# GpSimd computes the low part of 32 of 338 half slabs of weights

## The chip, the cores and the metric

The kernel runs on one core of a Trainium2 chip. A time is the device time of one execution in microseconds. Before the change it is 1015.32 us, the median of three runs (1015.02 to 1015.72). The profile shows one further execution. In its lines PE is TensorE's matmul, PEld its weight load, DVE is VectorE, ACT is ScalarE, POOL is GpSimd, and SP the engine whose queue issues the DMA transfers.

## The reference

The program is a decoder trunk of two layers on one sequence of 256 positions and width 1024, all in fp32. A layer is a feed-forward block, a mixer and a second feed-forward block, each with a modulated input and a residual with layer norm:

```python
mod = c_act @ mod_w[l] + mod_b[l]
sh1, sc1, g1, sh2, sc2, g2, sh3, sc3, g3 = jnp.split(mod, N_MOD, axis=-1)
f = swiglu(modulate(x, sh1, sc1), ffn_in[l, 0], ffn_out[l, 0])
x = deepnorm_residual(x, f, g1, ln_g[l, 0], ln_b[l, 0], 0.5)
u = modulate(x, sh2, sc2)
m = even_mixer(u, ...) if l % 2 == 0 else odd_mixer(u, positions, ...)
x = deepnorm_residual(x, m, g2, ln_g[l, 1], ln_b[l, 1])
f = swiglu(modulate(x, sh3, sc3), ffn_in[l, 1], ffn_out[l, 1])
x = deepnorm_residual(x, f, g3, ln_g[l, 2], ln_b[l, 2], 0.5)
```

The mixer of layer 0 ("even") joins a gated linear recurrence (RG-LRU, with a causal convolution in front) with chunked gated linear attention; that of layer 1 ("odd") is latent attention with 8 heads. The modulation vectors (shift, scale and gate of every block) are products of one conditioning vector with a large matrix.

## The kernel before

Activations lie transposed, 128 channels on the partitions by 256 positions, so every product has a 128 x 128 block of weights as the stationary operand. Each fp32 product is made of three products of a narrower form: the weight and the activation are both split into a high and a low part, and `mm3` issues high x high, high x low and low x high (L431, L432, L433). The activation parts are `uhi`, `ulo` for a block's input and `hhi`, `hlo` for the hidden layer.

The weights of the whole trunk stand in HBM in the order in which they are used (`PLAN`), in slabs of 16 blocks. `Stream` brings them: `dma_to` loads a slab of 1 MB into one of six raw buffers (`wraw`), from SP's queue; `conv_to` splits it in two half slabs of 128 x 1024 each. ACT copies the raw half slab into the high part (`whi`, L353, five buffers), and DVE subtracts that from the raw values to give the low part (`wlo`, L354, five buffers). The first slab is used unsplit, which leaves 338 half slabs to split. `next` hands out blocks and asks for the splits four half slabs ahead. A half slab feeds 24 matmuls.

The modulation products are not matmuls. `mods_to` loads two blocks of `modw` into one raw buffer, from the same queue and at a pace set by a table (`MOD_TARGETS`), and notes them in `todo`; `reduce` has DVE multiply such a 128 x 1024 block with the conditioning vector and add along the row (L405, tile `junk`, followed by a short accumulator read). `conv_to` calls it after a split when the first block noted is due, and twice when more than four are waiting.

The rest of DVE's work stands between: the hidden layer's product `h` (L818) and its split (L507), the layer norm (tiles `yy`, `acc`, `v`; class `Boundary`, where B of L631 is a folded modulation row), and the mixers. In the even mixer these are the key and query products (L1101, L1102, and L1108 with tile `la`), the recurrence's steps on four channel blocks at a time (`ya`, L978 to L987), and the residual (`xh`, L759). PE's L1075 there takes the scores of one head from `la`. `EVEN_STEPS` is the order of the even mixer's steps, one letter each: decays, values, keys, queries, gates and so on.

A scheduler decides in which order an engine's instructions stand, by priorities and by its own estimates of time; a few chains are tied by hand (`queue_behind`). Each engine then works through its queue in order, waiting on semaphores of the others. GpSimd has 24 instructions in this kernel, memsets and selects for constants and masks, none of which takes two inputs.

Of the kernel before, what the change touches and what calls it, by code (L numbers as in the profile page):

```python
# [11 lines left out]
F32 = mybir.dt.float32  # L12
# [7 lines left out]
MULT, ADD, SUB, MAX, MIN = ALU.mult, ALU.add, ALU.subtract, ALU.max, ALU.min  # L20
# [22 lines left out]

SH, SC, GT = 0, 1, 2
PRE, PREU = 4, 1
UOFF = 100
GOFF = 150
LVEC = (5, 6, 7)
# [187 lines left out]
def trunk_kernel(ctx: ExitStack, tc: tile.TileContext, xT, cvec, pos, wst, modw, colsd,  # L236
                 rgw, wa2, outT):
    nc = tc.nc
    sync, act, vec, pool, pe = nc.sync, nc.scalar, nc.vector, nc.gpsimd, nc.tensor
# [21 lines left out]
    def T(pl, shape, dt=F32, tag=None, **kw):  # L261
        return pl.tile(shape, dt, tag=tag, name=nm(tag), **kw)
# [12 lines left out]
    def axps():  # L275
        return T(ps_ax, [P, 512], tag="ax")
# [7 lines left out]
    def col(name, i, n=1):  # L284
        o = COLS[name][0]
        return cols[:, o + i:o + i + n]
# [18 lines left out]
    class Stream:  # L305
# [4 lines left out]
        def __init__(self):  # L310
            self.pos = 0
            self.raw = {}
            self.conv = {}
            self.ndma = 0
            self.nconv = 0
            self.nmod = 0
            self.todo = []
            self.behind = None
            self.pause = False
            self.ahead = Stream.AHEAD  # L320
            self.tight = False
            self.after = None
            self.modcols = {}
# [13 lines left out]
        def conv_to(self, n):  # L337

            self.dma_to((n - 1) // 2 + Stream.RAW)
            W2 = Stream.HS * P  # L340
            while self.nconv < min(n, 2 * NSLAB):
                s = self.nconv
                if s < 2 * RAWSLABS:

                    self.conv[s] = (self.raw[s // 2][:, (s % 2) * W2:(s % 2 + 1) * W2], None)
                    if s % 2:
                        self.raw.pop(s // 2)
                    self.nconv += 1
                    continue
                hi = T(whi, [P, W2], F32R, tag="whi")  # L350
                lo = T(wlo, [P, W2], F32R, tag="wlo")
                raw = self.raw[s // 2][:, (s % 2) * W2:(s % 2 + 1) * W2]
                ia = act.activation(hi, raw, AF.Copy)  # L353
                i = vec.tensor_tensor(lo, raw, hi.bitcast(F32), SUB)  # L354
                self.last_conv = ia, i
                if self.behind is not None:
                    queue_behind(i, self.behind)
                self.conv[s] = (hi, lo)
                if s % 2:
                    self.raw.pop(s // 2)  # L360
                self.nconv += 1
                if self.todo and not self.pause and self.todo[0][2] <= s // 2:
                    self.reduce()
                    if len(self.todo) > 4 and self.todo[0][2] <= s // 2:
                        self.reduce()
# [56 lines left out]
    W = Stream()  # L422
# [12 lines left out]
    def queue_behind(i, j):  # L435
        tc.add_manual_dep(i.ins, j.ins.name, mybir.DependencyInfo(
            mybir.DependencyClass.NoSync, mybir.DependencyReason.DATA), reason="order")
# [167 lines left out]
    class Boundary:  # L605
# [134 lines left out]
        def u(self, k):  # L740
# [3 lines left out]
            self.done.add(k)  # L744
            with tc.high_priority(offset=UOFF):
                if k >= PRE:
# [175 lines left out]
    def even(l, prev):  # L922
        with tc.tile_pool(name=nm("even"), bufs=1) as ep, tc.tile_pool(name=nm("ew"), bufs=2) as ew:
# [91 lines left out]
            def decays():  # L1015
                for h in range(GH):
                    hsl = slice(h * SEQ, (h + 1) * SEQ)
                    zp = axps()
                    pe.matmul(zp[:, :SEQ], wa2t[:, h * GDK:(h + 1) * GDK], za, start=True, stop=True)
                    act.activation(la[:, hsl], zp[:, :SEQ], AF.Abs, bias=col("gla_ba", h))  # L1020
                    vec.tensor_scalar(lb[:, hsl], zp[:, :SEQ], col("gla_ba", h), 0.0, ADD, MIN)
                ta(la, la, AF.Exp, scale=-1.0)
                ta(la, la, AF.Ln, bias=one_c)
                vec.tensor_tensor(la, lb, la, SUB)
                for h in range(GH):
                    hsl = slice(h * SEQ, (h + 1) * SEQ)
                    vec.tensor_tensor_scan(bc[:, hsl], scmask, la[:, hsl], 0.0, MULT, ADD)
                ta(la, bc, AF.Exp, scale=1.0 / 16)
                b3, lb3 = (t.rearrange("p (n e c) -> p n e c", e=2, c=GC) for t in (bc, lb))
                vec.tensor_copy(last, b3[:, :, :, GC - 1])  # L1030
                vec.tensor_copy(dec, la.rearrange("p (n e c) -> p n e c", e=2, c=GC)[:, :, :, GC - 1])
                ta(lb3[:, :, 1], b3[:, :, 1], AF.Exp, scale=-1.0 / 16)
                for e, t in ((0, lb3), (1, b3)):
                    vec.tensor_tensor(t[:, :, e], last[:, :, e:e + 1].broadcast_to([P, 2 * GH, GC]), b3[:, :, e], SUB)
                    ta(t[:, :, e], t[:, :, e], AF.Exp, scale=1.0 / 16)
                ta(b3[:, :, 0], b3[:, :, 0], AF.Exp, scale=-1.0 / 16)
# [105 lines left out]
                return yahi, yalo  # L1142

            for step in EVEN_STEPS:
                if step == "d": decays()
                elif step == "k": keys()
                elif step == "q": queries()
                elif step == "v": values()
                elif step == "A": gla_state()
                elif step in "OP": gla_out("OP".index(step))  # L1150
                elif step in "RS":
                    ta.use("exp_and_others")
                    rglru(4 * "RS".index(step))
                elif step == "g": sgg = gates()
                elif step == "a": yahi, yalo = rg_gates()
# [6 lines left out]

            with tc.high_priority(offset=UOFF):
                s8 = ss.rearrange("p t h -> p (t h)")
# [35 lines left out]
    def odd(l, prev):  # L1200
        with tc.tile_pool(name=nm("odd"), bufs=1) as op_, tc.tile_pool(name=nm("ow"), bufs=2) as ow:
# [63 lines left out]
            for half in range(2):  # L1265
                hi, lo = W.next(*[(("kv_up",), 0, ("v", 4 * half + c)) for c in range(4)])
# [66 lines left out]
            def queries(n):  # L1333
                for _ in range(n):
                    if ahead:
                        query(*ahead.pop(0))
# [4 lines left out]
            def output(f, ks):  # L1341
                if not first:
                    first.append(mmps())
                for k in ks:
                    mm3(first[0][:, :SEQ], W.next((("odd_out",), k, f)), (ohi[:, k, :], olo[:, k, :]),
                        k == 0, k == KD - 1)

            queries(4)
            for i in range(MH + 2):
                if i < MH:  # L1350
# [16 lines left out]
            for f in range(KD):  # L1367
                if f == 0:
                    ps = first[0]
                    output(0, range(6, KD))  # L1370
                    bd.tile_out(f, ps[:, :SEQ])
                    continue
                ps = mmps()
                for k in range(KD):
                    mm3(ps[:, :SEQ], W.next((("odd_out",), k, f)), (ohi[:, k, :], olo[:, k, :]),
                        k == 0, k == KD - 1)
                    if f == 1 and k == KD // 2:
                        bd.shift_out()
                bd.tile_out(f, ps[:, :SEQ])
        return bd  # L1380

    bd = None
# [99 lines left out]
```

## Time and profile before

| what | before |
|---|---|
| median of three runs | 1015.32 us |
| the profiled execution | 1015.46 us |
| its span, first to last instruction | 1013.7 us |
| TensorE busy, granted clock | 998.4 us, 0.997 |
| VectorE busy | 877.4 us |
| ScalarE busy | 611.9 us |
| GpSimd busy | 4.6 us |

The page gives for each engine its busy time within the span, and for groups of instructions with one line, operation and tiles their number, their busy time, the mean of one in ns, the idle time ahead of them and what ended it. Busy times overlap, as the engines run side by side. A wait is named by what released it.

### The profile page before, as it was taken

What the parts mean: (1) busy time and instruction counts of PE and PEld (TensorE: products, weight loads), DVE (VectorE), ACT (ScalarE), POOL (GpSimd) and SP (SyncE); (2) the same over time, 40 slices, a digit from 0 to 9 for tenths busy, and PEclk for the clock granted to TensorE, in tenths of its full rate; (3) what the DMA queues carried; (4) which work ended last, traced back from release to release, by engine and by line L of the source; (5) the groups of instructions that cost most, each with busy time, mean ns of one, the idle gap of its engine ahead of it and who ended that gap; (6) DMA issues with size and microseconds to landing.
All of it is one profiled execution on the core that took longest, in us unless ns stands there. A gap on an engine that the chain in (4) does not pass through costs nothing.

```text
span 1013.7 us, 20595 instructions
## 1 busy us (share of the span) xinstructions
PE 998.4 (98%) x8368; PEld 977.2 (96%) x8368; DVE 877.4 (87%) x1502; ACT 611.9 (60%) x1026; POOL 4.6 (0%) x24
## 2 busy tenths in 40 slices
PE   8999999999999999999999999999999999999997
PEld 7999999998999999999999999999999999999995
DVE  6889999798999999999986899999788799666664
ACT  5656665678895766655555674454569776454542
POOL 0000000000000000000000000000000000000000
PEclk9999999999999999999999999999999999999998
DMA  9998699554467954799976469998843156656501
GB/s 332 415 403 329 258 352 333 203 208 176 157 250 303 360 194 174 269 380 389 345 294 248 165 255 388 321 337 327 285 166 126 45 193 251 254 219 246 189 20 42
DMA packets 37999, 258.56 MB, mean 255 GB/s; under 512 B 4352, under 2 KB 5632, under 8 KB 7568
## 3 DMA queue, kind: packets, MB, share of 16 engines
q1 hardware_dynamic: 37904, 257.25, 67.5%
q8 instruction: 65, 1.06, 0.4%
q14 instruction: 30, 0.25, 0.1%
HBM read 256.18 MB, written 1.05 MB: 254 GB/s over the span
## 4 chain that ended last, share of the span: by engine, by line
PE 84%; DVE 9%; DMA 3%; issue 2%; ACT 2%; SPq 0%; DVEq 0%; ACTq 0%
PE mm L432 25%; PE mm L433 25%; PE mm L431 25%; DVE wlo L354 3%; DMA wraw<-modw 3%; DVE junk L405 1%; PE mm L1120 1%; PE mm L1119 1%; PE mm L1121 1%; ACT whi L353 1%; DVE flat L987 0%; PE ax L432 0%; PE ax L431 0%; PE ax L433 0%; PE mm L841 0%
## 5 line engine op out<-in xcount | busy, mean ns | idle before, releaser
L354 DVE TENSOR_TENSOR wlo<-wraw,whi 128x1024 fp32r<-128x1024 f32 x338 | 409.0, 1218 | 74.3 <-ACT whi L353 73.4
L353 ACT ACTIVATE whi<-wraw 128x1024 fp32r<-128x1024 f32 x338 | 355.2, 1057 | 192.6 <-PE mm L432 147.8
L431 PE MATMUL mm<-uhi,whi 128*128 128x256 f32 x1624 | 448.7, 277 | 0.8 <-DVE h L818 0.8
L432 PE MATMUL mm<-ulo,whi 128*128 128x256 f32 x1624 | 448.6, 277 | 0.1
L433 PE MATMUL mm<-uhi,wlo 128*128 128x256 f32 x1624 | 448.4, 277 | 0.0
L431 PEld LDWEIGHTS mm<-uhi,whi 128*128 128x128 f32 x1624 | 304.3, 188 | 1.4 <-ACT whi L353 1.0
L432 PEld LDWEIGHTS mm<-ulo,whi 128*128 128x128 f32 x1624 | 304.9, 188 | 0.6 <-DVE ulo L753 0.3
L433 PEld LDWEIGHTS mm<-uhi,wlo 128*128 128x128 f32 x1624 | 304.8, 188 | 0.1
L431 PE MATMUL mm<-hhi,whi 128*128 128x256 f32 x704 | 194.4, 276 | 0.0
L433 PE MATMUL mm<-hhi,wlo 128*128 128x256 f32 x704 | 194.4, 276 | 0.0
L432 PE MATMUL mm<-hlo,whi 128*128 128x256 f32 x704 | 194.4, 276 | 0.0
L405 DVE CUSTOM_DVE_ANT_0 junk<-wraw,cact,cols 128x1024 bf16<-128x1024 f32 x136 | 173.5, 1276 | 6.6 <-DMA wraw<-modw 6.2
L433 PEld LDWEIGHTS mm<-hhi,wlo 128*128 128x128 f32 x704 | 132.2, 188 | 0.0
L432 PEld LDWEIGHTS mm<-hlo,whi 128*128 128x128 f32 x704 | 132.2, 188 | 0.0
L431 PEld LDWEIGHTS mm<-hhi,whi 128*128 128x128 f32 x704 | 132.2, 188 | 0.0
L506 ACT ACTIVATE hhi<-h 128x256 fp32r<-128x256 f32 x88 | 36.0, 413 | 63.5 <-DVE h L818 63.5
L682 ACT ACTIVATE ysq<-yy 128x256 f32<-128x256 f32 x42 | 17.4, 415 | 44.6 <-DVE yy L678 44.1
L818 DVE SCALAR_TENSOR_TENSOR h<-mm,sg 128x256 f32<-128x256 f32 x75 | 30.8, 416 | 7.5 <-PE mm L433 7.5
L507 DVE TENSOR_TENSOR hlo<-h,hhi 128x256 fp32r<-128x256 f32 x88 | 36.1, 415 | 0.1
L678 DVE SCALAR_TENSOR_TENSOR yy<-mm,gate,ax 128x256 f32<-128x256 f32 x48 | 22.9, 478 | 14.9 <-PE mm L433 14.9
L453 ACT ACTIVATE sg<-mm 128x256 f32<-128x256 f32 x75 | 27.4, 366 | 5.0 <-PE mm L433 2.7
L431 PE MATMUL mm<-flat,whi 128*128 128x258 f32 x96 | 28.5, 296 | 0.0
(323 smaller groups left out, 1114.2 us busy)
## 6 DMA issues: line engine op xcount, KB each, us to landing
wraw<-wst SPq DMA_DIRECT2D x165, 1024.0 KB, 5.6
wraw<-modw SPq DMA_DIRECT2D x71, 1024.0 KB, 7.3
wraw<-wst SPq DMA_DIRECT2D x10, 512.0 KB, 10.6
wraw<-modw SPq DMA_DIRECT2D x2, 512.0 KB, 5.2
yy<-xT SPq DMA_DIRECT2D x8, 128.0 KB, 10.6
wraw<-rgw SPq DMA_DIRECT2D x1, 1024.0 KB, 4.8
outT<-yy SPq DMA_DIRECT2D x2, 256.0 KB, 2.8
outT<-yy SPq DMA_DIRECT2D x1, 512.0 KB, 2.6
```

What stands on the lines that cost most here:

```text
L353: ia = act.activation(hi, raw, AF.Copy)
L354: i = vec.tensor_tensor(lo, raw, hi.bitcast(F32), SUB)
L405: i = vec.tensor_tensor_reduce(junk, t, cact, 1.0, bias, MULT, ADD, self.modcols[(l, v)][:, j:j + 1])
L431: pe.matmul(ps, hi, mh, start=start, stop=False, skip_group_check=shared)
L432: pe.matmul(ps, hi, ml, start=False, stop=False, skip_group_check=shared)
L433: pe.matmul(ps, lo, mh, start=False, stop=stop, skip_group_check=shared)
L453: i = act.activation(out, in_, func, **kw)
L506: act.activation(hi, src, AF.Copy)
L507: return vec.tensor_tensor(lo, src, hi.bitcast(F32), SUB)
L678: vec.scalar_tensor_tensor(y, ps, self.gate[:, f:f + 1], ax[:, f, :], MULT, ADD)
L682: act.activation(ysq, y, AF.Square)
L818: vec.scalar_tensor_tensor(h, pu, bu, sg, ADD, MULT)
```

## The change

A counter runs over the half slabs that have company on DVE: those behind which a modulation sum is due, and those split while the mixers run, apart from the even mixer's steps d, g and a (decays and the two gates). Every third of these has its low part subtracted by GpSimd instead of DVE. ACT's high part, the raw data, the buffers and the matmuls are the same. It is 32 of the 338: 4 in the first feed-forward block, 8 in the even mixer and 20 behind it.

```diff
+SHARED = 3
@@ Stream.__init__
+            self.help = False
+            self.shared = 0
@@ Stream.conv_to
                 ia = act.activation(hi, raw, AF.Copy)
-                i = vec.tensor_tensor(lo, raw, hi.bitcast(F32), SUB)
+                due = self.todo and not self.pause and self.todo[0][2] <= s // 2
+
+                self.shared += bool(due or self.help)
+                by = pool if (due or self.help) and self.shared % SHARED == 0 else vec
+                i = by.tensor_tensor(lo, raw, hi.bitcast(F32), SUB)
...
-                if self.todo and not self.pause and self.todo[0][2] <= s // 2:
+                if due:
                     self.reduce()
@@ even()
             for step in EVEN_STEPS:
+                W.help = step not in "dga"
                 if step == "d": decays()
@@ odd()
+            W.help = True
             queries(4)
...
                 bd.tile_out(f, ps[:, :SEQ])
+            W.help = False
```

Lines behind the edit move by eight: L354 becomes L362, L431 to L433 become L439 to L441, L507 L515, L818 L826, L1075 L1083, L1108 L1116.

The first place is DVE's queue in the first feed-forward block, near 79 us of the trace. Before:

```order
L818 SCALAR_TENSOR_TENSOR h_173_1026<-mm_87_455,sg_172_1024 128x256
L354 TENSOR_TENSOR wlo_161_947<-wraw_134_742,whi_160_946 128x1024
L354 TENSOR_TENSOR wlo_165_979<-wraw_134_742,whi_164_978 128x1024
L507 TENSOR_TENSOR hlo_37_183<-h_171_1020,hhi_36_182 128x256
L507 TENSOR_TENSOR hlo_37_183<-h_173_1026,hhi_36_182 128x256
L818 SCALAR_TENSOR_TENSOR h_175_1032<-mm_88_456,sg_174_1030 128x256
```

With the change:

```order
L826 SCALAR_TENSOR_TENSOR h_173_1026<-mm_87_455,sg_172_1024 128x256
L362 TENSOR_TENSOR wlo_165_979<-wraw_134_742,whi_164_978 128x1024
L515 TENSOR_TENSOR hlo_37_183<-h_171_1020,hhi_36_182 128x256
L515 TENSOR_TENSOR hlo_37_183<-h_173_1026,hhi_36_182 128x256
L826 SCALAR_TENSOR_TENSOR h_175_1032<-mm_88_456,sg_174_1030 128x256
```

The first of two splits is gone from DVE; its row stands in GpSimd's queue.

The second place is DVE's queue in the even mixer, near 270 us, where the query products follow each other. Before:

```order
L354 TENSOR_TENSOR wlo_533_3351<-wraw_490_3093,whi_532_3350 128x1024
L1108 SCALAR_TENSOR_TENSOR la_461_2975<-mm_531_3349,la_461_2975 128x256
L759 SCALAR_TENSOR_TENSOR xh_534_3379<-yy_303_1819,ag_318_1847,r_405_2591 128x256
L354 TENSOR_TENSOR wlo_539_3388<-wraw_495_3127,whi_538_3387 128x1024
L1108 SCALAR_TENSOR_TENSOR la_461_2975<-mm_535_3382,la_461_2975 128x256
L759 SCALAR_TENSOR_TENSOR xh_540_3416<-yy_303_1819,ag_318_1847,r_405_2591 128x256
L354 TENSOR_TENSOR wlo_543_3421<-wraw_495_3127,whi_542_3420 128x1024
L1108 SCALAR_TENSOR_TENSOR la_461_2975<-mm_541_3419,la_461_2975 128x256
```

With the change:

```order
L362 TENSOR_TENSOR wlo_533_3351<-wraw_490_3093,whi_532_3350 128x1024
L1116 SCALAR_TENSOR_TENSOR la_461_2975<-mm_531_3349,la_461_2975 128x256
L767 SCALAR_TENSOR_TENSOR xh_534_3379<-yy_303_1819,ag_318_1847,r_405_2591 128x256
L1116 SCALAR_TENSOR_TENSOR la_461_2975<-mm_535_3382,la_461_2975 128x256
L767 SCALAR_TENSOR_TENSOR xh_540_3416<-yy_303_1819,ag_318_1847,r_405_2591 128x256
L362 TENSOR_TENSOR wlo_543_3421<-wraw_495_3127,whi_542_3420 128x1024
L1116 SCALAR_TENSOR_TENSOR la_461_2975<-mm_541_3419,la_461_2975 128x256
```

The split between the first and the second query product has left the queue.

The third place is TensorE's queue at the same point, where the scores of the four heads are taken in pairs of matmuls. Before, the second pair and the matmuls behind it:

```order
L1075 MATMUL ax_3493<-la_2975,bc_2977 128x64
L1075 MATMUL ax_3493<-la_2975,lb_2976 128x64
L431 MATMUL mm_3646<-uhi_161,whi_3350 128x256
L432 MATMUL mm_3646<-ulo_162,whi_3350 128x256
L433 MATMUL mm_3646<-uhi_161,wlo_3351 128x256
```

With the change, the second pair, the third and what follows:

```order
L1083 MATMUL ax_3493<-la_2975,bc_2977 128x64
L1083 MATMUL ax_3493<-la_2975,lb_2976 128x64
L1083 MATMUL ax_3493<-la_2975,bc_2977 128x64
L1083 MATMUL ax_3493<-la_2975,lb_2976 128x64
L439 MATMUL mm_3646<-uhi_161,whi_3350 128x256
L440 MATMUL mm_3646<-ulo_162,whi_3350 128x256
L441 MATMUL mm_3646<-uhi_161,wlo_3351 128x256
```

The third pair stood behind twelve matmuls and now follows the second at once; between the third and the fourth stand seven matmuls where fourteen stood.

## The prediction

> **What bounds the kernel now.** I read the head of the page first, then the chain of waits and the costliest groups.
>
> ```profile
> span 1013.7 us, 20595 instructions
> PE 998.4 (98%) x8368; PEld 977.2 (96%) x8368; DVE 877.4 (87%) x1502; ACT 611.9 (60%) x1026; POOL 4.6 (0%) x24
> PE 84%; DVE 9%; DMA 3%; issue 2%; ACT 2%; SPq 0%; DVEq 0%; ACTq 0%
> L354 DVE TENSOR_TENSOR wlo<-wraw,whi 128x1024 fp32r<-128x1024 f32 x338 | 409.0, 1218 | 74.3 <-ACT whi L353 73.4
> L405 DVE CUSTOM_DVE_ANT_0 junk<-wraw,cact,cols 128x1024 bf16<-128x1024 f32 x136 | 173.5, 1276 | 6.6 <-DMA wraw<-modw 6.2
> ```
>
> TensorE (PE) sets the time: 84% of the chain is matmul. VectorE (DVE) comes second, and two of its groups fill most of it: the low parts that the change touches (338 at 1.22 us) and the modulation sums. An average of 87% says little, so I cut the span into stretches. The columns are busy time (instructions) of PE, PEld, DVE, ACT, POOL, then clock and DMA.
>
> ```profile
> 60.00:100.00 40.00, 39.18 (x345) 39.01 (x344) 38.17 (x58) 22.91 (x37) 0.00 (x0) 1.00 0.90 353
> 100.00:180.00 80.00, 80.00 (x708) 80.00 (x707) 79.44 (x151) 47.66 (x75) 0.00 (x0) 1.00 0.84 315
> 250.00:300.00 50.00, 48.95 (x370) 46.62 (x369) 47.33 (x80) 44.00 (x92) 0.00 (x0) 1.00 0.57 207
> 300.00:350.00 50.00, 48.33 (x427) 48.12 (x426) 49.98 (x85) 34.01 (x60) 0.00 (x0) 1.00 0.83 317
> 460.00:560.00 100.00, 100.00 (x884) 100.00 (x883) 85.19 (x130) 51.98 (x73) 0.00 (x0) 1.00 0.82 311
> 560.00:660.00 100.00, 100.00 (x873) 99.46 (x872) 98.21 (x177) 57.17 (x95) 0.00 (x0) 1.00 0.77 289
> 860.00:1000.00 140.00, 140.00 (x1238) 140.00 (x1236) 88.31 (x117) 65.03 (x90) 0.00 (x0) 1.00 0.47 173
> ```
>
> DVE is full from 60 to 180, from 250 to 350 and from 560 to 660 us, and has room from 460 to 560 (85%) and after 860 (63%). Even where DVE is full, PE mostly runs without a hole. The lead explains it: a low part is finished some microseconds before PE reads it. Three pairs, each the split and the first matmul that reads it, show the lead where I found it thinnest:
>
> ```profile
> 118.82 1.22 DVE L354 TENSOR_TENSOR wlo<-wraw,whi 128x1024 fp32r<-128x1024 f32 x1
> 120.87 0.28 PE L433 MATMUL mm<-uhi,wlo 128*128 128x256 f32 x1
> 423.24 1.21 DVE L354 TENSOR_TENSOR wlo<-wraw,whi 128x1024 fp32r<-128x1024 f32 x1
> 425.54 0.28 PE L433 MATMUL mm<-uhi,wlo 128*128 128x256 f32 x1
> 662.81 1.22 DVE L354 TENSOR_TENSOR wlo<-wraw,whi 128x1024 fp32r<-128x1024 f32 x1
> 667.36 0.28 PE L433 MATMUL mm<-uhi,wlo 128*128 128x256 f32 x1
> ```
>
> The leads are 120.87 - 120.04 = 0.83 us, 1.09 us and 3.33 us. PE itself waits for DVE at only three places for more than half a microsecond after the start, and a little at the layer norm's sums of the odd mixer; these rows of its timeline end with the wait:
>
> ```profile
> 82.89 0.36 PE L431 MATMUL mm<-uhi,whi 128*128 128x256 f32 x1 [0.82 <-DVE h L818]
> 272.82 0.43 PE L1075 MATMUL ax<-la,bc 128*128 128x64 f32 x2 [1.05 <-DVE la L1108]
> 347.22 0.30 PE L1176 MATMUL ax<-ident,on 128*128 128x128 f32 x1 [1.67 <-DVE B L631]
> 819.00 0.67 PE L694 MATMUL ax<-acc,ones_dm 128*128 128x256 f32 x2 [0.41 <-DVE acc L685]
> ```
>
> **The change, part by part.** It takes 32 low parts from DVE's queue and puts them on GpSimd's (POOL). Matched by buffer to the splits of the trace, they stand at 58.6, 79.4, 106.4, 128.6 / 226.5, 236.6, 244.9, 260.5, 271.2, 283.6, 310.3, 333.5 / 419.0, 442.7, 462.1, 483.7, 511.3, 531.1 / 585.3, 607.6, 629.9, 658.6, 679.8, 702.7, 715.9 / 771.2, 789.0, 810.6, 817.3, 829.1, 885.1 and 920.4 us.
>
> What it removes: two splits in a row take 2.35 us on DVE (below), the second 1.21 of it, so one in a full queue is worth 1.14 us; 32 are 36 us of DVE time. No DMA, matmul or ACT instruction is added or taken away.
>
> ```profile
> 79.39 2.35 DVE L354 TENSOR_TENSOR wlo<-wraw,whi 128x1024 fp32r<-128x1024 f32 x2
> 82.33 0.74 DVE L818 SCALAR_TENSOR_TENSOR h<-mm,sg 128x256 f32<-128x256 f32 x2
> ```
>
> What it adds: 32 two-input subtractions on POOL, a form the trace does not have. The nearest rows:
>
> ```profile
> L938 POOL TENSOR_SCALAR_AFFINE_SELECT cmask<-cmask 128x512 int8<-128x512 int8 x1 | 0.6, 637 | 0.0
> L1251 POOL MEMSET kpe<- 128x512 f32 x1 | 0.5, 527 | 0.0
> L933 POOL MEMSET scmask<- 128x256 f32 x1 | 0.3, 312 | 192.5 <-PE mm L433 192.5
> ```
>
> From 256 to 512 elements a memset grows by 0.215 us, 0.84 ns per element. The select reads one input and writes 512 in 0.637; at 1024 that is 0.637 + 512 x 0.84 ns = 1.07 us, the lower bound (both inputs read at once). If the second input follows the first, 0.86 more: 1.93. If writing has its turn after both, 2.79, the upper bound. I take 1.93, since a select costs only 0.11 over a memset of its size: its reading and writing already overlap. [...]
>
> Latency alone hides. For the split at 106.4 ACT is done at 102.54 + 1.04 = 103.58, and PE first reads the result at 112.71: 9.1 us of cover for 1.93.
>
> ```profile
> 102.54 1.04 ACT L353 ACTIVATE whi<-wraw 128x1024 fp32r<-128x1024 f32 x1
> 112.71 0.28 PE L433 MATMUL mm<-uhi,wlo 128*128 128x256 f32 x1
> ```
>
> Without that cover the rest of the 1.93 would stand in front of PE. POOL's memsets for the mixers now queue behind a few of these splits, with as much room; SP's weight loads wait for POOL where they waited for DVE.
>
> So the question is whether DVE runs on while POOL works. One place speaks to it:
>
> ```profile
> 744.06 0.14 DVE L1214 TENSOR_SCALAR g<-cols 128x1 f32<-128x1 f32 x1
> 744.12 0.51 DVE L1215 TENSOR_SCALAR g<-cols 128x2 f32<-128x2 f32 x1
> 744.08 0.53 POOL L1251 MEMSET kpe<- 128x512 f32 x1
> ```
>
> DVE's two-column operation took 0.51 us where its one-column neighbour took 0.14, and it ended at 744.63, just behind POOL's memset (744.61). DVE was held for as long as POOL's instruction ran. I take it that a split on POOL, which reads two tensors, holds a DVE instruction that also reads two from SBUF, and in the full stretches nearly all do (splits, sums, hlo); h, with one input in PSUM, may pass. [...]
>
> Then each moved split costs a full DVE 1.93 - 1.14 = 0.79 us instead of saving 1.14.
>
> What it moves: the scheduler also reorders what stands near. In the even mixer PE's third pair of L1075 comes directly behind the second, where 12 matmuls stood between. Each pair waits for a query product (la), one per 1.87 us:
>
> ```profile
> 270.49 0.41 DVE L1108 SCALAR_TENSOR_TENSOR la<-mm,la 128x256 f32<-128x256 f32 x1
> 272.36 0.41 DVE L1108 SCALAR_TENSOR_TENSOR la<-mm,la 128x256 f32<-128x256 f32 x1
> 274.22 0.41 DVE L1108 SCALAR_TENSOR_TENSOR la<-mm,la 128x256 f32<-128x256 f32 x1
> ```
>
> In the new order the split between the first two la is gone, so they come 1.87 - 1.14 = 0.73 us apart and the next two 1.87 each, 4.47 in all. PE has three pairs (0.43 each, by the row at 272.82) and 7 matmuls (0.11 each, 708 in 80 us in the stretch from 100) to put in: some 2.1. It idles 2.4 us where it idled 1.05: 1.3 lost, whether or not anything is held. Its bounds are 0 (the matmuls passed over fill a later hole) and 2.4.
>
> **The sum.** Where PE already waits for DVE, lateness counts whole; elsewhere only above the lead.
> - 60 to 180: one split (79.4) ahead of the wait at 82.89: 0.8. Of the others one comes before the thin lead of 0.83 at 120: 0.79, just covered.
> - 250 to 350: 260.5 and 271.2 ahead of the wait at 272.82, then 283.6, 310.3 and 333.5 ahead of the one at 347.22: 5 x 0.79 = 4.0.
> - 400 to 460: one ahead of the lead of 1.09: covered. 560 to 740: four ahead of the lead of 3.33: 3.2, covered.
> - 800 to 860: 810.6 and 817.3 ahead of the sums for which PE waits at 819.00: 1.6.
> - Four (236.6, 244.9, 771.2, 789.0) stand in mixers where DVE has room, but PE follows chains that pass to and fro between ACT and DVE; a link that meets POOL waits half of 1.93 on average: 4 x 0.97 = 3.9.
> - The moved pair of L1075: 1.3.
> - The other 14 lie before idle DVE time or a lead: nothing.
>
> That is 11.6 us. Against the profiled execution's 1015.46 us (0.14 above the median of 1015.32) it gives **1027**. At 1.07 a hold saves as much as it costs, and only half of 1.07 in the four mixer places is left, with the 1.3: 1019. At 2.79 a split costs 1.65: 1.65 + 0.82 + 8.3 + 0.6 + 3.3 + 3.3 + 5.6 + 1.3 = 24.9, so 1040. [...]
>
> **Rivals.** (1) *POOL works beside DVE, nothing is held.* For it: at 196.18 a DVE instruction with two SBUF inputs starts 0.16 us before a reading POOL instruction ends, and takes 0.49 where its group's mean is 478 ns.
>
> ```profile
> 195.70 0.64 POOL L938 TENSOR_SCALAR_AFFINE_SELECT cmask<-cmask 128x512 int8<-128x512 int8 x1
> L651 DVE SCALAR_TENSOR_TENSOR flat<-yy,A,flat 128x256 fp32r<-128x256 f32 x40 | 18.9, 478 | 3.8 <-ACT flat L650 3.8
> 196.18 0.49 DVE L651 SCALAR_TENSOR_TENSOR flat<-yy,A,flat 128x256 fp32r<-128x256 f32 x1 [1.25 <-ACT flat L650]
> ```
>
> Against it: POOL may have read all it needed by then. DVE would gain 36 us, but PE only its waits, 0.8 + 1.05 + 1.67 = 3.5 at most, and less the 1.3 at L1075: 1012 to 1013.5, say 1012.5. (2) *DVE keeps the path.* If its back-to-back instructions go first each time, POOL waits; up to 9.1 us nothing shows, as each sum ends with an accumulator read that needs no tensor and lets POOL in. The holds and the relief then cancel: 1015.5, no change. (3) *Held, and worse than summed.* DVE's lateness also delays the release of the raw buffers and so the loads behind them (DMA is 0.8 busy in the full stretches); the leads that I let cover 0.8 + 0.8 + 3.2 us would be gone: 1027 + 4.8 = 1032. That the splits do not move is excluded by the order.
>
> **How the numbers follow.** Held as summed 0.44, worse 0.20, beside 0.28, cancelled 0.08. Alone, the likeliest has 1019 to 1040. Held cases are slower; of rival 1 a little falls short of 0.2%. About 0.2% (2 us) is what a measurement of this kernel tells from no change. Faster 0.25, same 0.11, slower 0.64. The range takes in rival 1 with some room below and the upper bound of the hold: 1010 to 1041.
>
> **What would show it.** Held: DVE's rows of 1.22 us (split) and 1.28 us (sum) stretch to some 2 to 3 us when they start during a POOL split, DVE's busy time rises though it has 32 fewer, and PE's waits at h, la and B grow. Beside: DVE's groups keep their means, its busy time falls by about 36 us, and those waits shrink. Either way POOL shows 32 rows whose mean is the price I estimated. Wrong at the root would be PE waiting for POOL's splits themselves, or a row far above 2.79 us.

## The result, and the profile after

The changed kernel takes 1042.83 us (median; 1040.45 to 1043.45), the kernel before 1015.69 in the same comparison: a ratio of 1.0263, 95% interval 1.0252 to 1.0274. It is 27 us slower. The prediction had 1027, within 1010 to 1041, and slower at 0.64. That it is slower, and that POOL holds DVE, was right. The size was too small by more than half, because of how the prediction counted the holds that reach PE.

The page of the changed kernel (span, busy time by engine, the chain of waits, the groups that answer to those of before; most lines are 8 further down; the splits of DVE and of POOL now share L362):

```profile
span 1038.7 us, 20666 instructions
PE 1007.9 (97%) x8368; PEld 982.5 (95%) x8368; DVE 896.8 (86%) x1470; ACT 608.1 (59%) x1026; POOL 91.6 (9%) x56
PE 64%; DVE 23%; issue 6%; ACT 3%; DMA 3%; SPq 0%; DVEq 0%; ACTq 0%
L362 DVE TENSOR_TENSOR wlo<-wraw,whi 128x1024 fp32r<-128x1024 f32 x306 | 375.6, 1236 | 69.7 <-ACT whi L357 68.9
L413 DVE CUSTOM_DVE_ANT_0 junk<-wraw,cact,cols 128x1024 bf16<-128x1024 f32 x136 | 192.4, 1415 | 8.7 <-DMA wraw<-modw 7.8
L362 POOL TENSOR_TENSOR wlo<-wraw,whi 128x1024 fp32r<-128x1024 f32 x32 | 87.0, 2719 | 752.7 <-ACT whi L357 617.9
```

DVE has 32 splits fewer and is busy for 896.8 us, 19.4 more than before. The sums went from a mean of 1276 ns to 1415. DVE's share of the chain went from 9% to 23%, PE's from 84% to 64%. POOL has no share of the chain: the trace names no instruction that waits for one of its 32 results, so the harm is not that they come late.

DVE's timeline shows where in its rows the time went. One POOL split, and what DVE did meanwhile (start, duration, engine, line, operation):

```profile
126.85 2.59 POOL L362 TENSOR_TENSOR wlo<-wraw,whi 128x1024 fp32r<-128x1024 f32 x1 [16.80 <-ACT whi L357]
127.09 3.43 DVE L413 CUSTOM_DVE_ANT_0 junk<-wraw,cact,cols 128x1024 bf16<-128x1024 f32 x1
```

POOL ends at 129.44. The sum starts at 127.09, takes 3.43 us instead of 1.28 and ends at 130.52, which is 1.08 behind POOL's end: nearly its whole work was done after POOL had finished. That is a hold for nearly the whole length of POOL's instruction, and not a slowdown of both.

PE's waits, from its timeline. They answer to the rows of before at 82.89 (0.82), 272.82 (1.05) and 819.00 (0.41); those at 145, 151, 163, 662 and 852 have no counterpart there. The wait at 347.22 (1.67, for B) shrank to 0.59 (for ut), at 361.48; ahead of it PE now waits 1.01 and 1.25 us for ACT, at 356.00 and 357.58:

```profile
84.51 0.36 PE L439 MATMUL mm<-uhi,whi 128*128 128x256 f32 x1 [2.68 <-DVE h L826]
145.01 0.39 PE L440 MATMUL mm<-hlo,whi 128*128 128x256 f32 x1 [1.09 <-DVE hlo L515]
151.08 0.39 PE L669 MATMUL ax<-shift,ones_r 128*128 128x256 f32 x1 [1.43 <-ACT shift L667]
163.39 0.39 PE L441 MATMUL mm<-hhi,wlo 128*128 128x256 f32 x1 [1.47 <-DVE wlo L362]
280.75 0.67 PE L1083 MATMUL ax<-la,bc 128*128 128x64 f32 x2 [2.21 <-DVE la L1116]
283.34 0.69 PE L1083 MATMUL ax<-la,bc 128*128 128x64 f32 x2 [0.64 <-DVE la L1116]
662.13 0.39 PE L441 MATMUL mm<-uhi,wlo 128*128 128x256 f32 x1 [1.17 <-DVE wlo L362]
840.66 1.19 PE L702 MATMUL ax<-acc,ones_dm 128*128 128x256 f32 x2 [2.53 <-DVE acc L693]
852.04 0.39 PE L440 MATMUL mm<-ulo,whi 128*128 128x256 f32 x1 [1.26 <-DVE ulo L761]
```

To see where 25 us were lost (the profiled execution took 1040.45, its span is 25.0 longer), I set the start of the n-th of PE's 8368 matmul records in the changed kernel against the n-th of before. The lag grows in steps. The table gives its growth by stretch of the kernel before, beside what the prediction charged there (its sum of 11.6), and the same for four kernels of the experiments below (ahead of 60 us the changed kernel gains 0.6, the others at most 0.3):

```
stretch (us of before)  forecast  changed  12 charged  6 covered  other 14  left out
 60 to 130                 0.8       2.9       1.2        0.0       1.3       0.1
130 to 180                 0         4.9       0.0        2.7       3.0       1.1
180 to 265                 1.9       0.0       0.2        0.0       0.0       0.1
265 to 300                 2.9       5.5       5.8        0.0       0.0      -0.3
300 to 400                 2.4       1.6       4.0        0.0       0.0      -1.9
400 to 640                 0         0.0       0.0        0.0       0.0       0.0
640 to 740                 0         3.4       0.0        2.4       0.0       0.0
740 to 810                 1.9       1.9       1.8        0.0       0.1      -0.6
810 to 860                 1.6       5.4       4.9        0.0       1.8      -0.7
behind 860                 0         0.0       0.0        0.0       0.0       0.0
```

One thing is new on PE itself. The granted clock falls to 0.50 twice ahead of the last microseconds, behind the waits of 2.21 us at 280.75 and of 2.53 at 840.66. Behind the longest wait, 2.68 at 84.51, it stays at 1.00 (windows of the changed kernel: PE, PEld, DVE, ACT, POOL busy, clock, DMA):

```profile
84.00:88.00 4.00, 3.49 (x29) 3.41 (x29) 4.00 (x9) 2.97 (x7) 0.00 (x0) 1.00 0.76 289
278.00:281.00 3.00, 0.79 (x7) 0.59 (x5) 3.00 (x6) 2.08 (x5) 0.00 (x0) 0.97 0.00 0
281.00:287.00 6.00, 5.36 (x25) 5.17 (x26) 5.09 (x11) 4.34 (x8) 0.00 (x0) 0.50 0.92 340
841.00:844.00 3.00, 2.81 (x7) 1.62 (x7) 2.06 (x5) 1.73 (x3) 0.00 (x0) 0.50 0.59 249
```

Before, the clock is at 1.00 in all stretches but the last 6 us. So there were three candidates for what made 27 of 11.6: the price of a hold, the places at which it counts, and the clock.

### The profile page after: what moved, and what is told of

The parts are those of the page before. It is cut to its first block, busy times and chain, and to the rows that moved or that the text cites. A ratio compares the mean times of both kernels' runs of the same rounds, so it can differ in the third digit from the quotient of the medians.

```text
span 1038.7 us, 20666 instructions
## 1 busy us (share of the span) xinstructions
PE 1007.9 (97%) x8368; PEld 982.5 (95%) x8368; DVE 896.8 (86%) x1470; ACT 608.1 (59%) x1026; POOL 91.6 (9%) x56
## 3 DMA queue, kind: packets, MB, share of 16 engines
HBM read 256.18 MB, written 1.05 MB: 248 GB/s over the span
## 4 chain that ended last, share of the span: by engine, by line
PE 64%; DVE 23%; issue 6%; ACT 3%; DMA 3%; SPq 0%; DVEq 0%; ACTq 0%
PE mm L440 19%; PE mm L439 19%; PE mm L441 19%; DVE wlo L362 7%; DVE junk L413 5%; DMA wraw<-modw 3%; DVE h L826 1%; DVE hlo L515 1%; ACT whi L357 1%; PE mm L1128 1%; PE mm L1127 1%; PE mm L1129 1%; DVE flat L659 1%; DVE flat L995 1%; DVE xh L767 1%
## 5 line engine op out<-in xcount | busy, mean ns | idle before, releaser
L439 PE MATMUL mm<-uhi,whi 128*128 128x256 f32 x1624 | 449.2, 278 | 2.7 <-DVE h L826 2.7
L441 PE MATMUL mm<-uhi,wlo 128*128 128x256 f32 x1624 | 450.2, 278 | 1.7 <-DVE wlo L362 1.6
L362 DVE TENSOR_TENSOR wlo<-wraw,whi 128x1024 fp32r<-128x1024 f32 x306 | 375.6, 1236 | 69.7 <-ACT whi L357 68.9
L439 PEld LDWEIGHTS mm<-uhi,whi 128*128 128x128 f32 x1624 | 304.9, 188 | 3.4 <-issue 3.1
L441 PEld LDWEIGHTS mm<-uhi,wlo 128*128 128x128 f32 x1624 | 305.6, 188 | 2.6 <-DVE wlo L362 2.5
L413 DVE CUSTOM_DVE_ANT_0 junk<-wraw,cact,cols 128x1024 bf16<-128x1024 f32 x136 | 192.4, 1415 | 8.7 <-DMA wraw<-modw 7.8
L441 PE MATMUL mm<-hhi,wlo 128*128 128x256 f32 x704 | 195.0, 277 | 1.5 <-DVE wlo L362 1.5
L439 PE MATMUL mm<-hhi,whi 128*128 128x256 f32 x704 | 194.8, 277 | 0.0
L362 POOL TENSOR_TENSOR wlo<-wraw,whi 128x1024 fp32r<-128x1024 f32 x32 | 87.0, 2719 | 752.7 <-ACT whi L357 617.9
L441 PEld LDWEIGHTS mm<-hhi,wlo 128*128 128x128 f32 x704 | 132.2, 188 | 1.9 <-DVE wlo L362 1.9
L439 PEld LDWEIGHTS mm<-hhi,whi 128*128 128x128 f32 x704 | 132.3, 188 | 0.0
L515 DVE TENSOR_TENSOR hlo<-h,hhi 128x256 fp32r<-128x256 f32 x88 | 41.7, 481 | 0.8 <-ACT hhi L514 0.8
L826 DVE SCALAR_TENSOR_TENSOR h<-mm,sg 128x256 f32<-128x256 f32 x75 | 31.1, 418 | 9.5 <-PE mm L441 9.4
## 6 DMA issues: line engine op xcount, KB each, us to landing
yy<-xT SPq DMA_DIRECT2D x8, 128.0 KB, 10.7
```

The lines of the kernel that those rows point to most:

```text
L362: i = by.tensor_tensor(lo, raw, hi.bitcast(F32), SUB)
L413: i = vec.tensor_tensor_reduce(junk, t, cact, 1.0, bias, MULT, ADD, self.modcols[(l, v)][:, j:j + 1])
L439: pe.matmul(ps, hi, mh, start=start, stop=False, skip_group_check=shared)
L441: pe.matmul(ps, lo, mh, start=False, stop=stop, skip_group_check=shared)
L515: return vec.tensor_tensor(lo, src, hi.bitcast(F32), SUB)
L826: vec.scalar_tensor_tensor(h, pu, bu, sg, ADD, MULT)
```

## The experiments

**Is it POOL at all?** First the 32 low parts left out on every engine, so that DVE is relieved and POOL does nothing (PLACES holds the numbers of the 32 half slabs):

```diff
-                i = vec.tensor_tensor(lo, raw, hi.bitcast(F32), SUB)
+                if s in PLACES:
+                    lo, i = hi, ia
+                else:
+                    lo = T(wlo, [P, W2], F32R, tag="wlo")
+                    i = vec.tensor_tensor(lo, raw, hi.bitcast(F32), SUB)
```

> The same 32 low parts are computed by no engine: for these half slabs PE's third matmul reads the high part instead (the output is another one), so DVE loses the 32 and POOL has nothing. Held (a reading POOL instruction stops DVE instructions with two SBUF inputs for its whole length): all of the loss is gone, and the relief shows only at the places where PE waits for DVE, 0.8 + 1.05 + 1.67 at most: 1012 to 1015. Rival, the loss comes from the changed order of instructions (third pair of L1075 and others) and not from POOL: slower than before, 1020 or more.

Measured: 1013.47 us, ratio 0.9974 (0.9965 to 0.9984). That is the whole worth of the relief, 2.0 us for 32 splits, near the 1012.5 of the prediction's first rival: -1.9 at the wait for B, -0.6 and -0.7 in the odd mixer and at the sums, +1.1 at 157. Set against this kernel, the changed one loses 29.4 us, and its DVE is busy for 50.2 us more (896.8 against 846.6): 1.57 us of hold for each split.

This kernel also has the order that the relief brings. On PE's timeline its third pair of the scores' matmuls stands directly behind the second too (L1079 here; the first row is the second pair, then the third and the fourth):

```profile
272.95 0.39 PE L1079 MATMUL ax<-la,bc 128*128 128x64 f32 x2
273.76 0.43 PE L1079 MATMUL ax<-la,bc 128*128 128x64 f32 x2 [0.20 <-DVE la L1112]
275.62 0.43 PE L1079 MATMUL ax<-la,bc 128*128 128x64 f32 x2 [0.31 <-DVE la L1112]
```

PE waits 0.20 us before the third pair and 0.31 before the fourth, less than the 1.05 of before: the 1.3 us of the prediction for the moved pair are not there. But another move does cost, one that the prediction did not look at. At 157 PE waits for a split that the new order of DVE puts later (PE's timeline):

```profile
157.50 0.39 PE L437 MATMUL mm<-hhi,wlo 128*128 128x256 f32 x1 [0.83 <-DVE wlo L358]
```

**What in a POOL instruction holds DVE?** Three kernels with all splits on DVE, and beside each of the 32 places one more POOL instruction that nobody waits for; the diff shows the three forms one after the other. But for the 880-column spare tile, the instructions of PE, DVE, ACT and SP and their order are those of before (with the memset a handful on DVE and ACT stand elsewhere).

```diff
                 i = vec.tensor_tensor(lo, raw, hi.bitcast(F32), SUB)
+                if s in PLACES:
+                    pool.tensor_tensor(spare, hi.bitcast(F32)[:, :880], hi.bitcast(F32)[:, :880], SUB)
...
+                    pool.tensor_copy(spare, hi.bitcast(F32)[:, :880])
...
+                    pool.tensor_copy(spare[:, :1], hi.bitcast(F32)[:, :1])
+                    pool.memset(spare, 0.0)
```

> The kernel before, with all low parts on DVE in the same order on every engine, and one POOL subtraction of 880 columns beside each of the 32 places, both inputs from the high part, result to a spare tile that nobody reads. Nobody waits for it, so only a hold can cost anything. POOL's split took 2.36 us unhindered for 1024 columns, so 880 take about 2.0. Held: DVE rows of 1.22 and 1.28 us reach 3.2 us, DVE's busy time rises by 32 x up to 2.0 = some 55 to 65 us, no relief stands against it, and the time goes to 1045 to 1065. Rival, the loss is PE waiting for late POOL results or the changed order: 1015.5, DVE's groups as before.

> As the run with the extra two-input subtraction, but the extra POOL instruction is a copy of 880 columns: one SBUF input. Held by whatever POOL reads: DVE is held for the copy's own length, about 0.9 to 1.2 us by the rows of the select (0.64 for 512), time 1025 to 1035. Rival, only two reads against two reads collide: no row of DVE is longer and the time is 1015.5.

> As the two runs with an extra POOL instruction, but it is a memset of the spare tile (880 columns, 0.53 + 368 x 0.84 ns = about 0.84 us), gated by a copy of one column: it writes and does not read. Held by reads alone: DVE's groups keep their means but for the short column copies, 1015.5 to 1018. Rival, any POOL instruction on SBUF holds DVE (as the memset of kpe beside the two-column row of L1215 seemed to say): DVE rows 0.8 us longer at the 32 places, 1023 to 1032.

Measured: two inputs 1045.42 us (ratio 1.0293, 1.0276 to 1.0311), one input 1026.16 (1.0111, 1.0091 to 1.0131), only written 1015.60 (1.0001, 0.9992 to 1.0011). DVE's busy time is 916.6, 893.1 and 878.2, against 877.4. The modulation sums on the page of the kernel with two inputs:

```profile
L409 DVE CUSTOM_DVE_ANT_0 junk<-wraw,cact,cols 128x1024 bf16<-128x1024 f32 x136 | 179.0, 1316 | 5.7 <-DMA wraw<-modw 5.4
```

of that with one input:

```profile
L409 DVE CUSTOM_DVE_ANT_0 junk<-wraw,cact,cols 128x1024 bf16<-128x1024 f32 x136 | 175.2, 1289 | 7.7 <-DMA wraw<-modw 7.3
```

and of that with the memset:

```profile
L410 DVE CUSTOM_DVE_ANT_0 junk<-wraw,cact,cols 128x1024 bf16<-128x1024 f32 x136 | 173.9, 1279 | 8.2 <-DMA wraw<-modw 7.9
```

Their means are 1316, 1289 and 1279 ns, where before has 1276. And one place of the last kernel's timeline, a memset on POOL beside a sum on DVE:

```profile
125.92 0.84 POOL L359 MEMSET spare<- 128x880 f32 x1
126.08 1.28 DVE L410 CUSTOM_DVE_ANT_0 junk<-wraw,cact,cols 128x1024 bf16<-128x1024 f32 x1
```

The sum takes its usual 1.28. So in these kernels the POOL instructions that read hold DVE (39.2 and 15.7 us more of its time), and the memset does not (0.8). With two reads a sum takes 2.67 us (at 129.32, beside POOL's row from 128.99 to 130.91), a hold of 1.39, where the POOL instruction takes 1.66 when nothing delays it: 0.27 less, where it is 0.25 in the changed kernel (2.15 against 2.40). With one read a sum takes 1.59 (at 128.41, beside POOL's row from 127.01 to 128.93), a hold of 0.31, where 0.52 of POOL's row was left. Both end 1.07 to 1.08 behind POOL, as the sum of the changed kernel does. So one read holds as two do here, and costs less time: the instruction takes 0.93 us against 1.66 when nothing delays it. That the memset does not hold also means that the row from which the prediction argued, the two-column operation of 0.51 us beside the memset of kpe, is no case of this hold, since that memset reads nothing. It takes 0.50 to 0.51 beside that memset in five traces (the kernel before, the changed one, the 32 left out, one input, memset), and what holds it was not tried.

These kernels rule out late POOL results and the order as the main cause. With two inputs DVE's time rose by less than the 55 to 65 us expected, 1.23 for each POOL subtraction of at least 1.66. 39.2 us more of DVE's time cost 29.9 us, and 15.7 cost 10.7: two thirds to three quarters of what was held reached the end in these two.

**Does the price go with the length?** POOL does 512 of the 1024 columns at the same 32 places, DVE the others:

```diff
+                H = W2 // 2
+                if s in PLACES:
+                    pool.tensor_tensor(lo[:, H:], raw[:, H:], hi.bitcast(F32)[:, H:], SUB)
+                    i = vec.tensor_tensor(lo[:, :H], raw[:, :H], hi.bitcast(F32)[:, :H], SUB)
+                else:
+                    i = vec.tensor_tensor(lo, raw, hi.bitcast(F32), SUB)
```

> All 32 places, but POOL does 512 of the 1024 columns and DVE the other 512. POOL's instruction should take half of 2.40, some 1.2 us, and a hold as long; DVE is relieved of some 0.5 instead of 1.14. Held: net 0.7 against 1.26 in a full queue, so somewhat over half of the loss and less of the slow clock behind PE's long holes, 1025 to 1031. Rival, the loss is a fixed one for each POOL instruction (a switch between the engines) and not its length: 1038 or more.

Measured: 1029.70 us, ratio 1.0141 (1.0126 to 1.0156), 14.2 us for half the columns and 27 for all, where POOL's instruction takes 1.29 us and 2.40 when nothing delays it. The loss goes with the length in these two kernels; a price for each POOL instruction that does not depend on its length is out.

**Which places count?** The 32 places in the three groups of the prediction's sum, each alone (PLACES with 12, 6 or 14 of the numbers):

```diff
-                i = vec.tensor_tensor(lo, raw, hi.bitcast(F32), SUB)
+                by = pool if s in PLACES else vec
+                i = by.tensor_tensor(lo, raw, hi.bitcast(F32), SUB)
```

> Only the 12 splits that the prediction charged go to POOL: 79.4, 236.6, 244.9, 260.5, 271.2, 283.6, 310.3, 333.5, 771.2, 789.0, 810.6 and 817.3. The prediction's accounting of places (only these cost): the whole loss, 1040 to 1043, stands here, and the other 20 are free. Accounting by the lag of the changed kernel's matmuls behind those of before, place by place (2.9 at 80, 5.1 at 275, 1.6 at 345, 1.8 in the odd mixer, about 5 at 815): 14 to 17 us, 1030 to 1033.

> Only the six splits go to POOL that the prediction held to be covered by a lead: 106.4, 419.0, 585.3, 607.6, 629.9 and 658.6. The prediction's accounting: 1015.5, within 0.2%. If leads are spent in a full stretch and a hold of 2.4 us takes 1.26 net: the one at 106.4 passes the lead of 0.83 by some 0.4, the four before 662 pass 3.33 by 1.7: 1017 to 1018.5. If they are worth nothing (DVE never makes up in a full stretch): 6 x 1.26 = 7.6, 1023.

> Only the other 14 go to POOL, which the prediction counted at nothing: 58.6, 128.6, 226.5, 442.7, 462.1, 483.7, 511.3, 531.1, 679.8, 702.7, 715.9, 829.1, 885.1 and 920.4. PE's order is that of before. The prediction's accounting: 1015.5. By the lag of the changed kernel: 128.6 lies before the 4.9 us lost at 140 to 160 and 829.1 before those at 835 to 850; what they cost alone is 0 to 5 us: up to 1020. Above 1020 the places between 440 and 535 and behind 860 would have to cost, where the lag of the changed kernel does not grow.

Measured: the 12 charged 1033.45 us (ratio 1.0174, 1.0159 to 1.0189), the 6 covered 1021.60 (1.0061, 1.0046 to 1.0076), the other 14 1022.04 (1.0069, 1.0052 to 1.0085). Above 1015.52 that is 17.9, 6.1 and 6.5, in all 30.5 where all together cost 27. So in these two kernels 12.6 us stand at places that the prediction had at nothing. All three times lie above what was expected from the lags (1030 to 1033, 1017 to 1018.5, up to 1020). Together the three lose more than the changed kernel. The largest difference is from 300 to 400: there the kernel with the 12 loses 4.0 and the changed one 1.6, and the clock of the first is at 0.50 from 352 to 358 of its trace, while that of the second stays at 1.00.

The lags say which places cost: 58.6 costs 1.3; 106.4 alone costs 2.7 and 128.6 alone 3.0, each at two waits, at 146 and 158; 829.1 costs 1.8. At 158 both groups lose 1.3, little more than the kernel with the 32 left out, which has no holds (1.1): that part looks like the order. The other eleven of the 14 cost nothing, as predicted. Of the 6, the three at 585.3, 607.6 and 629.9 together cost 2.4, from 640 to 646 of the kernel before, and 419.0 and 658.6 cost nothing: the loss is over before the POOL split of 658.6 starts. From the timelines of the kernel with the 6, two of POOL's rows, and a split of DVE between them with the matmul that waits for it:

```profile
635.29 2.92 POOL L356 TENSOR_TENSOR wlo<-wraw,whi 128x1024 fp32r<-128x1024 f32 x1 [21.77 <-ACT whi L354]
649.19 1.22 DVE L356 TENSOR_TENSOR wlo<-wraw,whi 128x1024 fp32r<-128x1024 f32 x1
650.46 0.38 PE L435 MATMUL mm<-uhi,wlo 128*128 128x256 f32 x1 [1.21 <-DVE wlo L356]
665.26 3.44 POOL L356 TENSOR_TENSOR wlo<-wraw,whi 128x1024 fp32r<-128x1024 f32 x1 [27.06 <-DVE hlo L509]
```

In the kernel before, the same split and the same matmul:

```profile
638.67 1.21 DVE L354 TENSOR_TENSOR wlo<-wraw,whi 128x1024 fp32r<-128x1024 f32 x1
645.60 0.28 PE L433 MATMUL mm<-uhi,wlo 128*128 128x256 f32 x1
```

There the split was done 5.7 us ahead of its reader.

**What does the slow clock cost?** The change written with the list of 32 numbers (same instructions, same order) as a second measurement, and the changed kernel with constant matmuls in the hole ahead of the scores' first pair:

```diff
                 sp = axps()
+                for _ in range(FILL if t == 0 else 0):
+                    pe.matmul(sp[:, :P], ones_dm, ones_dm, start=True, stop=True)
```

> The change written with a list of the 32 half slabs instead of the count: the instructions and their order on every engine are those of the changed kernel. It stands beside the next run on the same chip. Expected 1042 to 1043.5 under every theory; it says how far a time of the changed kernel moves from chip to chip.

> The changed kernel with 20 matmuls of constants (128 columns, 0.11 us each, 2.2 us in all; their result is overwritten) on PE directly ahead of the first pair that waits for la, where PE stands idle for 2.4 us in the changed kernel's trace and the granted clock is 0.50 for the 7 us behind. The fourth pair also comes up directly behind the third. If the slow clock is a price of its own, caused by the hole: the clock stays at 1.00 there and the time falls by 2 to 3.5 us against the run beside it. Rival, DVE sets the time in this stretch and the slow clock hides in PE's waits: no change, within 1 us, or slower by the matmuls that overrun the hole.

> As the run with 20 matmuls of constants, but 10: the trace of that run has 40 records of 0.11 us for its 20, so each takes 0.22 and they overran the hole by 2.1 us; 10 take 2.2 and fit. The order of PE is nearly that of the run with 20 (the fourth pair directly behind the third). If the slow clock is a price of its own: clock 1.00 from 276 to 290, and between the matmuls at 270 and 300 us (places of the kernel before) PE loses 3.3 us where the changed kernel loses 5.5, since part of the slow 7 us lies under a wait for the third la in any case. If it hides wholly under such waits: 5.5 again. The time also holds what the fourth pair's earlier place costs (a wait of 3.4 us for the scores in the run with 20): 1040 to 1043.

Measured: the change 1043.03 us (ratio 1.0274, 1.0260 to 1.0289), with 20 matmuls 1046.14 (1.0308, 1.0294 to 1.0322), with 10 1043.08 (1.0266, 1.0252 to 1.0280). The 20 were mis-sized, as the expectation of the next run says. With 10, the hole is full and the clock stays at 1.00 to 286 us; but the third and the fourth pair then wait for la in turn, 1.20 us each, and behind them the clock is at 0.50, from 287 to 293. PE's timeline of that kernel (the matmuls of constants, the third pair, the fourth):

```profile
279.99 2.39 PE L1083 MATMUL ax<-ones_dm 128*128 128x128 f32 x20
284.96 0.43 PE L1086 MATMUL ax<-la,bc 128*128 128x64 f32 x2 [1.20 <-DVE la L1119]
286.82 0.69 PE L1086 MATMUL ax<-la,bc 128*128 128x64 f32 x2 [1.20 <-DVE la L1119]
```

and two windows of it (columns as above):

```profile
280.00:286.00 6.00, 4.35 (x34) 3.76 (x32) 6.00 (x12) 5.47 (x11) 0.00 (x0) 1.00 0.49 157
287.00:293.00 6.00, 6.00 (x21) 5.30 (x21) 6.00 (x15) 1.47 (x4) 0.00 (x0) 0.50 0.31 130
```

The time did not fall, and PE loses 7.4 us from 265 to 300, more than either theory of that expectation had (3.3 and 5.5). DVE is busy in both windows without a gap, so it seems that DVE's chain sets the time here and that a faster PE would only wait longer. But the order moved as well (the fourth pair), so what the slow clock costs by itself stays open. It is not needed for the 12.6 us: the profiled executions of the 6 and of the 14 show no slow clock ahead of the last microseconds.

**What does POOL's time consist of?** The extra subtraction in two forms in turn, since the first had taken less per column than the changed kernel's own:

```diff
+                if s in PLACES:
+                    a, b = (raw, spare) if PLACES.index(s) % 2 else (hi.bitcast(F32), spare.bitcast(F32R))
+                    pool.tensor_tensor(b, a[:, :880], hi.bitcast(F32)[:, :880], SUB)
```

> The kernel before with an extra POOL subtraction of 880 columns at the 32 places, in two forms in turn: 16 read the high part twice and write fp32r, 16 read raw and high and write fp32. Read twice and written as fp32 it took 1.66 us unhindered, and the changed kernel's own (raw and high, fp32r, 1024 columns) 2.36, which is 2.03 for 880. If the type written costs the difference, the first 16 take 2.0 and the second 1.66; if two different sources do, the other way round. Time about that of the run with the extra two-input subtraction, 1045 to 1050.

Measured: 1053.09 us (one execution), above the 1045 to 1050 expected. Of each form an instruction that nothing delayed, from POOL's timeline:

```profile
433.48 1.66 POOL L359 TENSOR_TENSOR spare<-whi 128x880 fp32r<-128x880 f32 x1 [81.73 <-ACT whi L355]
729.14 2.09 POOL L359 TENSOR_TENSOR spare<-wraw,whi 128x880 f32<-128x880 f32 x1 [19.70 <-ACT whi L355]
```

Two different sources take 0.43 us more than one source read twice. The type written made no difference: one source read twice takes 1.66 with fp32r here and 1.66 with fp32 in the kernel with the extra subtraction.

## Why the prediction was right or wrong

**What bounds the kernel, and that DVE is held: right.** DVE's rows stretch as announced (3.43 for 1.28), its busy time rises with 32 instructions fewer, PE's waits at h and la grow (that for B shrinks), and the kernels with extra POOL instructions show the hold without any relief or other order. The row that the prediction read as a hold was none of this kind, so that part was lucky. Rivals 1 and 2 (POOL beside DVE, or cancelling) are out. Rival 1's row at 196.18 does not speak against the hold: it starts 0.16 us before POOL's row ends, and the held operation of its kind at 836.31 (below) ends 0.29 behind POOL's row with 0.48 of work, so it begins 0.19 before that row's end. POOL's results were never late, also as said.

**The price of a split on POOL: mis-sized, but not what was missing.** The step was "I take 1.93", within 1.07 and 2.79. Undelayed rows of POOL's timeline in the changed kernel give 2.36 to 2.40:

```profile
427.70 2.40 POOL L362 TENSOR_TENSOR wlo<-wraw,whi 128x1024 fp32r<-128x1024 f32 x1 [78.18 <-ACT whi L357]
807.64 2.36 POOL L362 TENSOR_TENSOR wlo<-wraw,whi 128x1024 fp32r<-128x1024 f32 x1 [16.30 <-DVE nmx L1305]
```

The 1.93 fits an instruction whose two sources are one tensor (1.66 for 880 columns, 1.93 for 1024 in proportion); a second tensor costs more, and that was not in the estimate. With 2.40 the net of a split is 1.26 instead of 0.79, and the prediction's own sum becomes 1.26 + 0.43 + 6.3 + 0.17 + 1.7 + 2.5 + 4.8 + 1.3 = 18.5, 7 us more of the 15 that were missing. But that takes every hold at POOL's full time, and the traces do not show it: a full hold of a sum is 2.15, the average is 1.57, and DVE's busy time rose by 19.4 us, 0.61 net for each split, less than the 0.79. So most of what was missing lies in how holds were counted, in the next two steps.

**"Just covered" and "the other 14: nothing": the first step that failed.** Charged even with 2.40, the 6 covered splits come to 2.3 us (0.43 + 0.17 + 1.7) and the 14 to nothing; measured are 6.1 and 6.5, of which the order may be 1.1 in each. I read three leads of the kernel before and let each stand for its stretch. The lead at 120 did hold (the lag does not grow from 100 to 140), but a DVE that is full until 180 stays late, and at 146 the lead was thinner, 0.41 us. In the kernel before, ACT's shift of the layer norm and PE's matmul that reads it:

```profile
144.97 0.42 ACT L659 ACTIVATE shift<-yy 128x256 fp32r<-128x256 f32 x1 [1.35 <-DVE yy L678]
145.80 0.28 PE L661 MATMUL ax<-shift,ones_r 128*128 128x256 f32 x1
```

The other places were not thinner. In the kernel before, the hlo for which the changed kernel waits at 145.01 was done 3.3 us ahead of its reader, the split of 163.39 6.6, that of 662.13 5.7. At all four DVE's order changed too, so the leads of before are not those of the changed kernel. The new order without holds (the 32 left out) loses 1.1 at 158 and nothing at 141, at 146 and from 640 to 646, so there the holds are needed. How much of each lead they took and how much the order took was not separated. Where DVE has room (440 to 560, behind 860) the rule did hold.

**Relief set against the hold, net of 0.79 at a wait: the second step that failed.** In the kernel with the 12 charged splits DVE's busy time rose by 10.3 (887.7 against 877.4), 0.86 for each, near the 0.79. The time rose by 17.9, 1.49 for each. The sums of the odd mixer show why. At 810 to 860 the two charged splits were to cost 1.6 and cost 4.9. The hold falls on the last instructions of the chain for which PE waits. The timelines of POOL and DVE in the changed kernel:

```profile
835.80 2.84 POOL L362 TENSOR_TENSOR wlo<-wraw,whi 128x1024 fp32r<-128x1024 f32 x1 [7.81 <-DVE yy L686]
836.31 2.62 DVE L659 SCALAR_TENSOR_TENSOR flat<-yy,A,flat 128x256 fp32r<-128x256 f32 x1
838.85 0.41 DVE L694 TENSOR_TENSOR acc<-acc,ysq 128x256 f32<-128x256 f32 x1
```

An operation of 0.48 us became one of 2.62, 2.14 lost right ahead of acc. The 1.14 of relief cannot be set against that: the left-out kernel shows that relief is worth 0.7 in this stretch. Gross hold where PE waits, and relief only where DVE would have been late, are two sums and not one difference. The other charged places were not taken apart in this way.

**The mixers: half right.** The two places of the odd mixer cost 1.8, as charged (1.9). The two of the even mixer at 236.6 and 244.9 cost 0.2 together, not 1.9.

**The moved order: the wrong place.** The pair at L1075 costs nothing by itself (0.20 and 0.31 of wait with the same order and no hold). The split at 157, which I had not compared, costs 1.1.

**265 to 300**: 5.8 in the kernel with the 12 alone, against 1.6 + 1.3 predicted. Holds in front of la explain more than was charged, the slow clock lies in the same microseconds, and the two were not separated.

**Rival 3 (held and worse, leads gone)** came nearest in kind. Of its two reasons the leads are shown. Late loads are not: the sums' wait for their DMA is 7.8 us in all, against 6.2 before.

## What to carry to other kernels

Before work with two SBUF inputs goes from DVE to POOL, find out what DVE does in that time. If it too reads two tensors from SBUF, a POOL instruction that reads can hold it for nearly its whole length, here 2.15 us of 2.40 for a sum that meets it early and 1.57 on average. The subtraction itself took 2.4 us on POOL and 1.2 on DVE here, so a full DVE lost. Measure the relief alone first by leaving the work out; here that showed in one run that there were 2 us to win. And a lead read at one place says nothing for its stretch: take the least over all places down to where the late engine next has room, and read it in the order that the changed kernel will have. Where PE already waits, do not set the relief against the hold.

## What the runs showed of the hardware that was not expected

- POOL is delayed as well. Its row at 105.92 starts 0.02 us behind a split of DVE and takes 4.13 us, and the mean over the 32 is 2719 ns, where an undelayed one takes 2.40. In that row's time DVE got through the split (1.22), an hlo (0.42), an h (0.42) and an operation that reads PE's result `mm` (0.68) at their usual lengths; only the next hlo was held (2.02 for 0.42).
- POOL on 880 columns, undelayed: memset 0.84 us, one-input copy 0.93, subtraction of one source from itself 1.66, of two sources 2.09.
- PE's granted clock fell to 0.50 behind a hole of 2.2 us (at 278.5 to 280.75) for 7 us, but not behind the one of 2.68 us ahead of 84.51 in the same kernel, and not behind one with a wait of 3.09 at 352 in the kernel with the extra copy. Its row on PE's timeline:

```profile
352.41 0.30 PE L1180 MATMUL ax<-ident,on 128*128 128x128 f32 x1 [3.09 <-DVE B L635]
```

and the windows there:

```profile
349.00:353.00 4.00, 0.91 (x8) 0.70 (x7) 4.00 (x11) 2.88 (x7) 0.00 (x0) 1.00 0.97 373
353.00:357.00 4.00, 4.00 (x37) 4.00 (x36) 4.00 (x10) 2.63 (x4) 0.00 (x0) 1.00 1.03 412
```

The length of one hole does not decide it in these traces; what does was not tried.
